# Returning the last expert pair's results inside the next norm's loop, with the branch for full experts ahead of that pair's down products

## The chip, the cores and the metric

The kernel runs on one core of a Trainium2 chip. The metric is the device time of one execution in microseconds (us). The core has five engines with queues of their own, each of which works strictly in the order of its program: PE (TensorE, matrix products; its weight loads are listed as PEld), DVE (VectorE), ACT (ScalarE), POOL (GpSimd) and SP (SyncE, which here only issues transfers). Engines wait for one another through semaphores.

## The reference

Two layers over x of 512 tokens by 1024 channels, float32. Layer 0 mixes the tokens with differential attention, layer 1 with stick-breaking attention, and a mixture of 32 experts follows each. Ahead of each of the four sub-layers x is normed by rows and modulated; behind it the result, times a gate, is added to x. At the end x is normed once more, with a gain:

```
def rms_norm(x, g, eps=RMS_EPS):
    xf = x.astype(jnp.float32)
    y = xf * lax.rsqrt(jnp.mean(xf * xf, axis=-1, keepdims=True) + eps)
    return (y * g.astype(jnp.float32)).astype(x.dtype)
```

Each token goes to the best two experts of the best of four groups, and each expert is `silu(x @ gate) * (x @ up) @ down`, weighted by its probability. No assignment is dropped, however many tokens choose one expert.

## The kernel before

**Tiles and pairs.** The 512 tokens are four tiles of 128 (`NT`), tile i of x being `xt(xs, i)`. `experts` (called once for each layer) works on the 32 experts in 16 pairs, 64 places for each expert. For a pair, `gate_up` makes gate and up products, `act_mul` the hidden values, `hid_transposed` turns them, `down` makes the down products (L1229, 16 products that the trace shows as 32, since each float32 product takes two passes), `slot_weights` and `slot_tokens` the matrix that maps places to tokens (its last operation is L1202 on DVE), and `scaled_parts` scales the result from PSUM (DVE, L1050) and splits it in two parts that the faster matrix format holds: `hi` on ACT (L1059) and `lo`, the remainder, on DVE (L1060).

**The return.** `combine` (L1069 and L1072) returns a group's results to the tokens: for one tile and one half of the channels, PE multiplies the place matrix by `hi` and by `lo` (L1069), and DVE adds the product to x (L1072). For the last pair that is 4 tiles x 2 halves, 16 products and 8 additions.

**The branch.** `overflow` (L1082) handles tokens beyond an expert's 64 places. It stands in a branch of the program that every engine takes together: each loads the count `nb` (L1088), and jumps over the body if it is zero (L1090), which it is in both layers of the profiled execution. No instruction is moved over the branch, and an engine leaves it only when the others' work before it that it depends on is done.

**The next norm.** After layer 0 the norm of layer 1 is done tile by tile in `norm_modulate_tile` (L451): the sum of squares on ACT (L400), the root on ACT (L404), a reciprocal and a Newton step of eight small operations for two tiles on DVE (L405 to L414), a diagonal matrix of the result (L456, DVE), 8 products that scale and transpose the tile at once (L460, PE, 16 passes in the trace), the modulation from PSUM (L469 on DVE, L467 on ACT), and again a split in `hi` (L472, ACT) and `lo` (L473, DVE). The first products of layer 1's attention (L556 to L558, its v projection, 24 for each tile) need these parts, and the split of their weights (L484 on ACT, L485 on DVE). x itself goes to the buffer `x2d` in memory (L1283). After layer 1 the final norm is done tile by tile (L1436 to L1445), and the last half tile's transfer to `out` ends the program.

**The order.** The order of each engine's program is made when the kernel is built: instructions are recorded, and a scheduler places each by what it depends on, within what `behind` and `chain` fix by hand. A branch closes such a stretch. The weights come over SP's queue in a fixed order (`fetch`, `release`, `reserve`); the last pair's down weights are 8 loads of 512 KB.

Of the kernel before, what the change touches and what calls it, by code (L numbers as in the profile page):

```python
# [9 lines left out]
F32 = mybir.dt.float32  # L10
# [27 lines left out]
def trunk_kernel(ctx: ExitStack, tc: tile.TileContext, io):  # L38
# [78 lines left out]
    def sl(s):  # L117
        return slots[:, s, :]
# [74 lines left out]
    def behind(inst, *others):  # L193
        for other in others:
            tc.add_manual_dep(inst.ins, other.ins.name, no_sync, reason="lesser work comes later")
# [203 lines left out]
    def row_sumsq(x_ap, junk, out):  # L399
        act.activation(junk, x_ap, AF.Square, accum_out=out)  # L400
# [50 lines left out]
    def norm_modulate_tile(i, xs, cols, ring4, ring2):  # L451
        ssq = small.tile([P, 1], F32, name="ssqt")
        row_sumsq(xt(xs, i), ring4(), ssq)
        r = rstd_of(ssq, 1, 1e-6, D)
        diag = ring2()[:, 0:P]
        diags.append(dve.tensor_scalar(diag, ident, r[:, 0:1], None, op0=ALU.mult))  # L456
        pt = sc_ps()
        full = ring4().rearrange("p (kb t) -> p kb t", kb=KB)
        for kb in range(KB):
            pe.matmul(pt[:, kb // 4, P * (kb % 4):P * (kb % 4) + P], lhsT=xt(xs, i)[:, P * kb:P * kb + P], rhs=diag,  # L460
                      start=(kb % 4 == 0), stop=(kb % 4 == 3))
        for kb in range(KB):
            c, j = kb % 4, kb // 4
            po = pt[:, j, P * c:P * c + P]
            a, b = cols[:, c, 2 + j:3 + j], cols[:, c, j:j + 1]
            if kb % 2:
                act.activation(full[:, kb, :], po, AF.Identity, scale=a, bias=b)  # L467
            else:
                dve.tensor_scalar(full[:, kb, :], po, a, b, op0=ALU.mult, op1=ALU.add)  # L469
        for j in range(2):  # L470
            hi, lo = (rs_(s[j]).rearrange("p (kb t) -> p kb t", kb=4)[:, :, P * i:P * i + P] for s in (R_HI, R_LO))
            last_a = act.activation(hi, full[:, 4 * j:4 * j + 4, :], AF.Copy)  # L472
            last_d = dve.tensor_tensor(lo, full[:, 4 * j:4 * j + 4, :], hi.bitcast(F32), op=ALU.subtract)  # L473
        return last_a, last_d


# [686 lines left out]
    def experts(l, st, xs, g2, hte_sl, w2, r2, ap, shp, rows, wrows):  # L1163
# [56 lines left out]
        def down(hidT):  # L1220
            pd = sc_ps()
            for hf in range(2):
                ws = [fetch(), fetch()]
                for f2 in range(2):
                    fb = 2 * hf + f2
                    for nn in range(2):
                        for e in range(2):
                            c0 = 1024 * f2 + 512 * nn
                            chain(pe.matmul(pd[64 * e:64 * e + 64, nn, :], lhsT=hidT[:, fb, 64 * e:64 * e + 64],  # L1229
                                            rhs=sl(ws[e])[:, c0:c0 + 512], start=(fb == 0), stop=(fb == 3)))  # L1230
                release(ws)
            return pd

        group = []
        for pr in range(np_):
            if pr == np_ - 1:
                reserve(5)
            pg = gate_up(pr)
            if pr == 0:
                wt = route_weights(st, w2, md)  # L1240
                token_rows(lambda c, i: st["sid"][:, c, i:i + 1], lambda: (r2(), ones_r), rows, (md,), True)
                token_rows(lambda c, i: wt[:, i, c:c + 1], lambda: (w2(), ones), wrows, (), True)
                sidq = small.tile([P, nq, 2, NT], F32, name="sidq", bufs=1)
                for qd in range(nq):
                    behind(dve.tensor_scalar(sidq[:, qd], st["sid"], float(-256 * qd), None, op0=ALU.add), md)
                ovf = route_overflow(st, w2)
            hid = act_mul(pg, slice(0, P), w2)
            units = []
            if pr % 2 and pr < np_ - 1:
                units = [lambda k2=k2: dispatch(k2) for k2 in range(KB // 2)]  # L1250
            elif pr:
                done, group = group, []
                units = [lambda i=i, nn=nn: combine(done, xs, i, nn) for i in range(NT) for nn in range(2)]
            if pr == np_ - 1:

                behind(act.activation(small.tile([P, 1], F32, name="table"), eps6, AF.Sqrt), *silu)
            half = len(units) // 2
            for u in units[:half]:
                u()
            hidT = hid_transposed(hid, P, w2, chain)  # L1260
            for u in units[half:]:
                u()
            pd = down(hidT)
            slotw = slot_weights(pr)
            group.append((slot_tokens(pr), scaled_parts(pd, slotw, g2, w2, r2)))
            if pr % 2 == 0 and pr < np_ - 2:
                for i in range(NT):
                    pick(sidq, i, pr // 2 + 1, sb, w2)
        overflow(l, st, ovf, wt, xs, g2, ap, shp, rows)
        for i in range(NT):  # L1270
            for nn in range(2):
                combine(group, xs, i, nn)


    sbs = [None]
    x2d = dram.tile([S, D], F32, name="x2d")
    for l in range(2):
        if l == 0:
            xsrc = x_v
        else:  # L1280
            xsrc = x2d.rearrange("(t p) d -> p t d", p=P)
            for s2 in range(2):
                nc.sync.dma_start(xsrc[:, 2 * s2:2 * s2 + 2, :], sl(x_sl[s2]).rearrange("p (t d) -> p t d", t=2))  # L1283
            xo_sl = alloc(2)
            work_sl = alloc(4)
        w4 = Ring(parts_of(slots, work_sl[0:3], 1024))
        w2 = Ring(parts_of(slots, work_sl[3:4], 512))
        if l == 0:
            ada_flush((0, 0), 2)
            neglam, sgc = late_loads()  # L1290
            norm_transposed(x_sl, xo_sl, w4)
        else:
            for i in range(NT):
                anchor[:] = norm_modulate_tile(i, x_sl, columns[1, 0], w4, w2)
        reserve(4)
        release(x_sl)
# [13 lines left out]
                order = ((0, 0), (1, 0), (0, 1), (1, 1), (2, 0), (2, 1))  # L1310
            units.append((g, order))
        linked.clear()
        holds = {(0, 2): (None, diags[1]), (0, 0): anchor} if l else {}
        line = Line([u for g, order in units for u in qkv_units(l, g, qkv_sl, order, chain)], holds)
        line.split(1)
        if l == 0:
# [106 lines left out]
        reserve(0)  # L1423
        w2 = Ring(parts_of(slots, work_sl[0:1], 512))
        rows, wrows = parts_of(rslots, (R_ROWS,), 512)[0:2], parts_of(slots, r_sl, 512)[0:2]
        experts(l, st, x_sl, g2, hte_sl, w2, r2, ap, shp, rows, wrows)
        reserve(8)
        release(hte_sl + r_sl + work_sl[0:1])

# [4 lines left out]
    ov = io["out"].rearrange("o (t p) d -> p (o t) d", p=P)  # L1434
    w4 = Ring(parts_of(slots, alloc(2), 1024))
    for i in range(NT):  # L1436
        ssq = small.tile([P, NT], F32, name="ssq")
        t = w4()
        row_sumsq(xt(x_sl, i), t, ssq[:, 0:1])
        r = rstd_of(ssq, 1, 1e-6, D)  # L1440
        n = 2 if i == NT - 1 else 1
        for c in range(n):
            cs_ = slice(D // n * c, D // n * c + D // n)
            dve.scalar_tensor_tensor(t[:, cs_], xt(x_sl, i)[:, cs_], r[:, 0:1], gf[:, cs_], op0=ALU.mult, op1=ALU.mult)  # L1444
            nc.sync.dma_start(ov[:, i, cs_], t[:, cs_])  # L1445


# [24 lines left out]
```

## Time and profile before

| | |
|---|---|
| median of 3 runs | 1587.94 us (1587.5 to 1588.52) |
| the profiled execution's own time | 1587.79 us |
| its span, first to last instruction | 1586.1 us |
| PE busy | 1510.2 us (95%) |
| DVE busy | 819.1 us (52%) |
| ACT busy | 456.2 us (29%) |
| POOL busy | 69.8 us (4%) |
| mean granted TensorE clock | 0.978 of full speed |

The span is 1.7 us shorter than the execution's own time; this lies around the span. Busy times overlap, so they don't add up to it. Layer 0 ends near 796 us, where the last L1229 of its experts is done, and layer 1's near 1564 us.

### The profile page before, as it was taken

The numbers are of one execution on the slowest core, as the hardware profiler recorded it, in microseconds if no ns is written. First come the engines' busy times: TensorE is split into PE (matmuls) and PEld (weight loads), VectorE is DVE, ScalarE is ACT, GpSimd is POOL, SyncE is SP. The second block draws the span as 40 slices with busy tenths as digits, with TensorE's granted clock in tenths as the row PEclk, the third lists the DMA queues.
The fourth block names the chain that finished last, engine by engine and source line by source line (L and its number), as shares of the span: only waits on it lengthen the run. The fifth ranks groups of instructions, "written<-read, shape, count | busy, mean of one in ns | idle before, by whom it ended". The sixth has DMA issues, their size and how long they took to land. (4 is left out here: it accounts for less than half of the span.)

```text
span 1586.1 us, 20509 instructions
## 1 busy us (share of the span) xinstructions
PE 1510.2 (95%) x8077; PEld 910.2 (57%) x8077; DVE 819.1 (52%) x1664; ACT 456.2 (29%) x830; POOL 69.8 (4%) x98
## 2 busy tenths in 40 slices
PE   4999989899999999999989999998999999999996
PEld 2887778754544545544467877885445545445542
DVE  5957845743443442442477787666342343343345
ACT  4564655521111101101164545453101111111112
POOL 0000000000000000000002223300000000000000
PEclk8999999989999999999989999998999999999997
DMA  9837734179999999999966455323999999999994
GB/s 379 314 130 273 257 132 156 40 262 418 421 421 421 422 420 422 421 421 421 399 211 239 147 186 187 133 88 122 415 421 421 420 422 421 421 421 421 421 414 169
DMA packets 111519, 501.63 MB, mean 316 GB/s; under 512 B 14832, under 2 KB 39440, under 8 KB 65336
## 3 DMA queue, kind: packets, MB, share of 16 engines
q1 hardware_dynamic: 109688, 498.01, 79.1%
q10 hardware_dynamic: 1728, 2.23, 0.4%
q8 instruction: 67, 1.10, 0.3%
q14 instruction: 36, 0.29, 0.1%
HBM read 495.97 MB, written 4.23 MB: 315 GB/s over the span
## 5 line engine op out<-in xcount | busy, mean ns | idle before, releaser
L1214 PE MATMUL banks<-slots 128*64 128x512 f32 x2048 | 453.1, 595 | 0.2 <-DMA slots<-in_expert_w_up_dram 0.2
L1214 PEld LDWEIGHTS banks<-slots 128*64 128x64 f32 x2048 | 156.3, 138 | 290.6 <-issue 276.4
L1229 PE MATMUL banks<-slots 128*64 128x512 f32 x1024 | 226.8, 595 | 1.4 <-ACT slots L1046 1.4
L1037 DVE TENSOR_TENSOR slots<-slots,banks 128x512 f32<-128x512 f32 x32 | 22.0, 687 | 272.3 <-PE banks L1214 272.3
L1069 PE MATMUL banks<-rslots 128*128 128x512 f32 x512 | 142.8, 424 | 10.6 <-DVEq L1090 5.3
L1229 PEld LDWEIGHTS banks<-slots 128*64 128x64 f32 x1024 | 70.7, 137 | 137.3 <-issue 130.6
L1050 DVE SCALAR_TENSOR_TENSOR slots<-banks,slotw,slots 128x512 f32<-128x512 f32 x64 | 45.1, 746 | 191.8 <-PE banks L1229 186.1
L1069 PEld LDWEIGHTS banks<-rslots 128*128 128x128 f32 x512 | 91.3, 194 | 62.6 <-DVE slots L1072 25.9
L1059 ACT ACTIVATE rslots<-slots 128x512 fp32r<-128x512 f32 x64 | 40.0, 631 | 301.3 <-DVE slots L1050 300.0
L1182 PEld LDWEIGHTS banks<-hot,rslots 128*128 128x128 f32 x896 | 109.1, 192 | 11.4 <-issue 11.4
L1182 PE MATMUL banks<-hot,rslots 128*128 128x256 f32 x896 | 114.5, 286 | 0.0
L1072 DVE TENSOR_TENSOR slots<-banks,slots 128x512 f32<-128x512 f32 x144 | 97.2, 688 | 25.6 <-PE banks L1069 25.6
L539 PE MATMUL banks<-rslots 128*128 128x512 f32 x256 | 104.0, 406 | 3.7 <-ACT rslots L447 3.7
L540 PE MATMUL banks<-rslots 128*128 128x512 f32 x256 | 100.9, 394 | 0.8 <-DVE rslots L448 0.8
L541 PE MATMUL banks<-rslots 128*128 128x512 f32 x256 | 100.9, 394 | 0.0
L485 DVE TENSOR_TENSOR rslots<-slots,rslots 128x1024 fp32r<-128x1024 f32 x64 | 78.2, 1234 | 27.5 <-ACT rslots L484 26.0
L934 ACT ACTIVATE slots<-banks,consts 128x256 f32<-128x256 f32 x64 | 35.6, 564 | 197.2 <-PE banks L1182 174.9
L331 DVE SCALAR_TENSOR_TENSOR slots<-slots,consts 128x1024 f32<-128x1024 f32 x70 | 87.4, 1281 | 7.0 <-DMA slots<-in_ada_w_dram 6.9
L484 ACT ACTIVATE rslots<-slots 128x1024 fp32r<-128x1024 f32 x64 | 66.9, 1056 | 58.6 <-PE banks L540 20.5
L556 PE MATMUL banks<-rslots 128*128 128x256 f32 x256 | 74.5, 291 | 0.7 <-ACT slots L545 0.6
L558 PE MATMUL banks<-rslots 128*128 128x256 f32 x256 | 73.2, 286 | 0.5 <-DVE rslots L473 0.5
L557 PE MATMUL banks<-rslots 128*128 128x256 f32 x256 | 73.1, 286 | 0.0
(240 smaller groups left out, 1920.1 us busy)
## 6 DMA issues: line engine op xcount, KB each, us to landing
slots<-in_expert_w_gate_dram SPq DMA_DIRECT2D x104, 1024.0 KB
slots<-in_expert_w_up_dram SPq DMA_DIRECT2D x104, 1024.0 KB
slots<-in_expert_w_down_dram SPq DMA_DIRECT2D x104, 1024.0 KB
slots<-in_ada_w_dram SPq DMA_DIRECT2D x48, 1024.0 KB
slots<-in_expert_w_gate_dram SPq DMA_DIRECT2D x48, 512.0 KB
slots<-in_expert_w_up_dram SPq DMA_DIRECT2D x48, 512.0 KB
slots<-in_expert_w_down_dram SPq DMA_DIRECT2D x48, 512.0 KB
slots<-in_diff_w_in_dram SPq DMA_DIRECT2D x12, 1024.0 KB
```

The costliest lines, as they stand in the source:

```text
L331: add = dve.scalar_tensor_tensor(acc[:, c_], sl(s)[:, c_], cs[:, kb:kb + 1], acc[:, c_], op0=ALU.mult, op1=ALU.add)
L485: j = dve.tensor_tensor(rs_(ls)[:, cs_], sl(s)[:, cs_], rs_(hs)[:, cs_].bitcast(F32), op=ALU.subtract)
L539: link(pe.matmul(pt, lhsT=wh[:, kb, :], rhs=rT(R_HI, kb), start=(kb == 0), stop=False))
L540: link(pe.matmul(pt, lhsT=wh[:, kb, :], rhs=rT(R_LO, kb), start=False, stop=False))
L541: link(pe.matmul(pt, lhsT=wl[:, kb, :], rhs=rT(R_HI, kb), start=False, stop=(kb == KB - 1)))
L556: link(pe.matmul(po, lhsT=rT(R_HI, kb, ts), rhs=wh[:, kb, :], start=(kb == 0), stop=False))
L558: link(pe.matmul(po, lhsT=rT(R_LO, kb, ts), rhs=wh[:, kb, :], start=False, stop=(kb == KB - 1)))
L1069: chain(pe.matmul(pt, lhsT=sT[:, P * i:P * i + P], rhs=parts[nn][part], start=(n + part == 0), stop=(n == len(group) - 1 and part == 1)))
L1072: dve.tensor_tensor(xn, pt, xn, op=ALU.add)
L1182: chain(pe.matmul(pt[:, 256 * kk:256 * kk + 256], lhsT=rT(r, kb, slice(P * i, P * i + P)), rhs=sb[:, i, :], start=(i == 0 and r == R_HI), ...
L1214: chain(pe.matmul(pg[64 * e:64 * e + 64, w, :], lhsT=hTe[:, kb, c0:c0 + 64], rhs=sl(ws[e])[:, 512 * kk:512 * kk + 512], start=(kb == 0), s ...
L1229: chain(pe.matmul(pd[64 * e:64 * e + 64, nn, :], lhsT=hidT[:, fb, 64 * e:64 * e + 64], rhs=sl(ws[e])[:, c0:c0 + 512], start=(fb == 0), sto ...
```

## The change

In each layer's last pair, the place matrix and the branch now come ahead of `down`, with the small operation that loads ACT's table for the square root behind the branch (it stood ahead of `hid_transposed`). `experts` no longer returns the last pair's results itself. It gives back a function `last(i)` that does so for tile i; the caller runs it at the start of each turn of the next norm's loop. In layer 1 the store of x to `x2d` follows tile by tile in that loop. In `norm_modulate_tile` the diagonal and `lo` go to GpSimd. In the final norm, tiles 0 and 1 are scaled on ACT and multiplied by the gain on GpSimd; tiles 2 and 3 stay on DVE, in halves.

```diff
@@ norm_modulate_tile
-        diags.append(dve.tensor_scalar(diag, ident, r[:, 0:1], None, op0=ALU.mult))
+        pool.tensor_scalar(diag, ident, r[:, 0:1], None, op0=ALU.mult)
...
-                dve.tensor_scalar(full[:, kb, :], po, a, b, op0=ALU.mult, op1=ALU.add)
+                last_d = dve.tensor_scalar(full[:, kb, :], po, a, b, op0=ALU.mult, op1=ALU.add)
...
-            last_d = dve.tensor_tensor(lo, full[:, 4 * j:4 * j + 4, :], hi.bitcast(F32), op=ALU.subtract)
+            pool.tensor_tensor(lo, full[:, 4 * j:4 * j + 4, :], hi.bitcast(F32), op=ALU.subtract)
+        diags.append(last_d)
         return last_a, last_d
@@ experts
-            if pr == np_ - 1:
-
-                behind(act.activation(small.tile([P, 1], F32, name="table"), eps6, AF.Sqrt), *silu)
...
-            pd = down(hidT)
-            slotw = slot_weights(pr)
-            group.append((slot_tokens(pr), scaled_parts(pd, slotw, g2, w2, r2)))
+            if pr == np_ - 1:
+
+                slotw, sT = slot_weights(pr), slot_tokens(pr)
+                overflow(l, st, ovf, wt, xs, g2, ap, shp, rows)
+
+                behind(act.activation(small.tile([P, 1], F32, name="table"), eps6, AF.Sqrt), *silu)
+                pd = down(hidT)
+            else:
+                pd = down(hidT)
+                slotw, sT = slot_weights(pr), slot_tokens(pr)
+            group.append((sT, scaled_parts(pd, slotw, g2, w2, r2)))
...
-        overflow(l, st, ovf, wt, xs, g2, ap, shp, rows)
-        for i in range(NT):
+        def last(i):
             for nn in range(2):
                 combine(group, xs, i, nn)
+        return last
@@ layer 1, norm ahead of attention
-            for s2 in range(2):
-                nc.sync.dma_start(xsrc[:, 2 * s2:2 * s2 + 2, :], sl(x_sl[s2]).rearrange("p (t d) -> p t d", t=2))
...
             for i in range(NT):
+                last(i)
+                nc.sync.dma_start(xsrc[:, i, :], xt(x_sl, i))
                 anchor[:] = norm_modulate_tile(i, x_sl, columns[1, 0], w4, w2)
...
-        holds = {(0, 2): (None, diags[1]), (0, 0): anchor} if l else {}
+        holds = {(0, 2): (None, diags[0]), (0, 0): anchor} if l else {}
@@ final norm
     for i in range(NT):
-        ssq = small.tile([P, NT], F32, name="ssq")
+        last(i)
+        ssq = small.tile([P, 1], F32, name="ssqt")
         t = w4()
-        row_sumsq(xt(x_sl, i), t, ssq[:, 0:1])
+        row_sumsq(xt(x_sl, i), t, ssq)
         r = rstd_of(ssq, 1, 1e-6, D)
-        n = 2 if i == NT - 1 else 1
-        for c in range(n):
-            cs_ = slice(D // n * c, D // n * c + D // n)
+        if i < 2:
+            act.activation(t, xt(x_sl, i), AF.Copy, scale=r[:, 0:1])
+            pool.tensor_tensor(t, t, gf, op=ALU.mult)
+            nc.sync.dma_start(ov[:, i, :], t)
+            continue
+        for c in range(2):
+            cs_ = slice(512 * c, 512 * c + 512)
             dve.scalar_tensor_tensor(t[:, cs_], xt(x_sl, i)[:, cs_], r[:, 0:1], gf[:, cs_], op0=ALU.mult, op1=ALU.mult)
-            nc.sync.dma_start(ov[:, i, cs_], t[:, cs_])
+            if i == NT - 1 or c:
+                at = cs_ if i == NT - 1 else slice(0, D)
+                nc.sync.dma_start(ov[:, i, at], t[:, at])
```

In the changed kernel the lines from L457 to about L1250 have numbers one higher, so that L1069, L1072, L1229 and L485 of before are L1070, L1073, L1230 and L486; the orders below keep each kernel's own numbers. The rows between the jump and the end of the branch's body, which is not run, are left out.

First, PE at the end of layer 0, before:

```order
L1069 MATMUL banks<-rslots 128x512 x8
L1044 MATMUL banks<-consts,slots 128x128 x4
L1069 MATMUL banks<-rslots 128x512 x8
L1229 MATMUL banks<-slots 64x512 x16
L1088 TENSOR_LOAD nb
L1090 COMPARE_AND_BRANCH
...
L1090 UNCONDITIONAL_BRANCH
L1069 MATMUL banks<-rslots 128x512 x16
L460 MATMUL banks<-slots 128x128 x16
L556 MATMUL banks<-rslots 128x256
```

and in the change:

```order
L1070 MATMUL banks<-rslots 128x512 x8
L1045 MATMUL banks<-consts,slots 128x128 x4
L1070 MATMUL banks<-rslots 128x512 x8
L1089 TENSOR_LOAD nb
L1091 COMPARE_AND_BRANCH
...
L1091 UNCONDITIONAL_BRANCH
L1230 MATMUL banks<-slots 64x512 x16
L1070 MATMUL banks<-rslots 128x512 x16
L460 MATMUL banks<-slots 128x128 x24
L557 MATMUL banks<-rslots 128x256
```

The last pair's down products have moved behind the branch, and three tiles of the norm's products, where there were two, stand ahead of the first 22 v products; the fourth tile's follow these.

Second, ACT at the same place, before:

```order
L1256 ACT_TABLE_LOAD
L1256 ACTIVATE table<-consts 128x1
L1046 ACTIVATE slots<-banks 128x512
L1059 ACTIVATE rslots<-slots 128x512
L1088 TENSOR_LOAD nb
L1090 COMPARE_AND_BRANCH
...
L1059 ACT_TABLE_LOAD
L1059 ACTIVATE rslots<-slots 128x512
L484 ACTIVATE rslots<-slots 128x1024 x2
L400 ACTIVATE slots,ssqt<-slots 128x1024
L404 ACT_TABLE_LOAD
L404 ACTIVATE rstd<-ssqt,consts 128x1
```

and in the change:

```order
L1047 ACTIVATE slots<-banks 128x512
L485 ACTIVATE rslots<-slots 128x1024
L1089 TENSOR_LOAD nb
L1091 COMPARE_AND_BRANCH
...
L1266 ACT_TABLE_LOAD
L1266 ACTIVATE table<-consts 128x1
L485 ACTIVATE rslots<-slots 128x1024
L1060 ACTIVATE rslots<-slots 128x512 x2
L400 ACTIVATE slots,ssqt<-slots 128x1024
L404 ACTIVATE rstd<-ssqt,consts 128x1
```

Both halves of `hi` now stand behind the branch, no table load stands among them or ahead of the first root, and one split of v weights (L485, L484 of before) stands ahead of the branch. At the end of layer 1 ACT's order is the same without the two splits.

Third, GpSimd in layer 1's norm, in the change (before, only the fills L696 stood there):

```order
L456 TENSOR_SCALAR slots<-consts,rstd 128x128 x3
L473 TENSOR_TENSOR rslots<-slots,rslots 128x4x128 x2
L696 MEMSET slots 128x2
L473 TENSOR_TENSOR rslots<-slots,rslots 128x4x128
L696 MEMSET slots 128x2
L473 TENSOR_TENSOR rslots<-slots,rslots 128x4x128
L696 MEMSET slots 128x2
L456 TENSOR_SCALAR slots<-consts,rstd 128x128
L473 TENSOR_TENSOR rslots<-slots,rslots 128x4x128 x2
```

The fourth tile's diagonal (L456) stands behind the first two tiles' four subtractions (L473).

## Rows read from the trace of the kernel before

**Rows 1.** Windows: each engine's busy time, granted clock and DMA share, layer 1.
```profile
core 0: us, PE busy (x) PEld busy (x) DVE busy (x) ACT busy (x) POOL busy (x), PEclk, DMA share, GB/s
830.00:900.00 70.00, 69.31 (x394) 54.97 (x393) 57.03 (x60) 35.91 (x52) 20.55 (x23) 1.00 0.60 211
1200.00:1550.00 350.00, 348.53 (x1744) 168.14 (x1744) 131.60 (x254) 43.29 (x73) 0.00 (x0) 1.00 1.01 420
```

**Rows 2.** Timeline of PE, end of layer 0 and start of layer 1.
```profile
start us, us, engine line op out<-in xcount [idle before <-releaser]
788.52 7.09 PE L1229 MATMUL banks<-slots 128*64 128x512 f32 x32
798.22 1.01 PE L1069 MATMUL banks<-rslots 128*128 128x512 f32 x2 [2.62 <-DVEq L1090]
808.45 5.46 PE L460 MATMUL banks<-slots 128*128 128x128 f32 x32 [1.80 <-DVE slots L456]
817.69 3.74 PE L460 MATMUL banks<-slots 128*128 128x128 f32 x32
821.18 0.36 PE L558 MATMUL banks<-rslots 128*128 128x256 f32 x1
829.89 0.28 PE L558 MATMUL banks<-rslots 128*128 128x256 f32 x1
```

**Rows 3.** Timeline of DVE, the same stretch.
```profile
789.23 0.74 DVE L1202 SCALAR_TENSOR_TENSOR rslots<-rslots,consts,slots 128x512 fp32r<-128x512 f32 x1
795.72 1.41 DVE L1050 SCALAR_TENSOR_TENSOR slots<-banks,slotw,slots 128x512 f32<-128x512 f32 x2 [5.75 <-PE banks L1229]
797.17 0.69 DVE L1060 TENSOR_TENSOR rslots<-slots,rslots 128x512 fp32r<-128x512 f32 x1
800.19 0.68 DVE L1072 TENSOR_TENSOR slots<-banks,slots 128x512 f32<-128x512 f32 x1
806.68 0.69 DVE L1072 TENSOR_TENSOR slots<-banks,slots 128x512 f32<-128x512 f32 x1 [0.15 <-PE banks L1069]
808.12 0.48 DVE L456 TENSOR_SCALAR slots<-consts,rstd 128x128 f32<-128x128 f32 x2
808.51 1.22 DVE L485 TENSOR_TENSOR rslots<-slots,rslots 128x1024 fp32r<-128x1024 f32 x1
```

**Rows 4.** Timeline of ACT, the same stretch.
```profile
785.99 0.60 ACT L1046 ACTIVATE slots<-banks 128x512 f32<-128x512 f32 x1 [8.17 <-PE banks L1044]
799.46 1.99 ACT L484 ACTIVATE rslots<-slots 128x1024 fp32r<-128x1024 f32 x2
803.10 1.28 ACT L404 ACT_TABLE_LOAD   x1
804.60 1.04 ACT L400 ACTIVATE slots<-slots 128x1024 f32<-128x1024 f32 x1
805.97 1.04 ACT L400 ACTIVATE slots<-slots 128x1024 f32<-128x1024 f32 x1
```

**Rows 5.** Windows, the last pair's return at the end of layer 0.
```profile
799.20:807.50 8.30, 6.97 (x15) 3.31 (x14) 6.24 (x13) 7.44 (x13) 0.00 (x0) 0.64 0.32 126
```

**Rows 6.** Line L670 on GpSimd and on DVE: durations in ns, minimum/median/maximum.
```profile
L670 POOL TENSOR_TENSOR slots<-slots,rs x6: 1040/1040/1042, 112.2 to 217.1; 128x512 f32<-128x512 f32 x6
L670 DVE TENSOR_TENSOR slots<-slots,rs x2: 691/691/691, 248.4 to 267.3; 128x512 f32<-128x512 f32 x2
```

**Rows 7.** Timeline of DVE, end of the program: after the last down products.
```profile
1564.10 1.41 DVE L1050 SCALAR_TENSOR_TENSOR slots<-banks,slotw,slots 128x512 f32<-128x512 f32 x2 [5.75 <-PEq L1090]
1580.90 1.41 DVE L1444 SCALAR_TENSOR_TENSOR slots<-slots,rstd 128x512 f32<-128x512 f32 x2
```

**Rows 8.** Timeline of SP, transfers issued at both ends.
```profile
770.79 10.31 SPq L133 DMA_DIRECT2D slots<-in_expert_w_down_dram  x8
791.49 0.35 SPq L136 DMA_DIRECT2D slots<-in_ada_w_dram  x1
1577.60 5.07 SPq L1445 DMA_DIRECT2D out_dram<-slots  x5
```

More of the change, by code (lines that the diff above doesn't have):

```diff
@@ L1425, in trunk_kernel @@
         rows, wrows = parts_of(rslots, (R_ROWS,), 512)[0:2], parts_of(slots, r_sl, 512)[0:2]
-        experts(l, st, x_sl, g2, hte_sl, w2, r2, ap, shp, rows, wrows)
+        last = experts(l, st, x_sl, g2, hte_sl, w2, r2, ap, shp, rows, wrows)
         reserve(8)
```

## The prediction

> **What bounds the kernel now.** I read the windows first. In layer 1's attention and over its experts PE is busy 99% of the time at a granted clock of 1.00 [rows 1]; the transfers are full beside it in the experts, but the list of waits has none of PE on them there. So a microsecond that PE gains before 830 us should still be there at the end, and one that it loses too. Next come the two ends, in the timelines. In this text T is the start of the first scaling L1050, right behind the last L1229: 795.72 in layer 0 [rows 3], 1564.10 in layer 1 [rows 7].
>
> Behind T, PE waits 2.62 us at the branch [rows 2]. The first addition to x starts at 800.19, T + 4.47, the last ends at 807.37, T + 11.65 [rows 3]; ACT loads a table for 1.28 us between the first sum of squares and its root [rows 4], and the clock averages 0.64 in the stretch [rows 5]. L460 starts at 808.45, T + 12.7, and the 96 v products, with the norm's last two tiles between them, end at 829.89 + 0.12, T + 34.3 [rows 2]. At the end of the program the last scaling by DVE ends at 1582.31, T + 18.2 [rows 7], and the span 3.8 us later, for the last half tile's store and the end of the program. These two lengths, 34.3 and 18.2 us, are what the change can shorten.
>
> **The cost: the branch before the down products.** It now stands where PE would go straight on. DVE comes to it only behind L1202, which ends at 789.97 [rows 3]. From the end of DVE's last operation before the branch (797.17 + 0.69) to PE's first product behind it (798.22) took 0.36 us [rows 2, 3], so the down products go on at 790.33. All but the first two now stand behind DVE's branch; the third started at 788.52 + 2 x 0.22 = 788.96. That is 1.4 us later. The same operations stand at the end of layer 1, so I count it twice: **+2.8 us**. Nothing hides it, since PE stands on the path there. Bounds: 0.9 (the products that run early cover part) and 3.6 us (0.4 more at each branch, as long again as the 0.36).
>
> ACT must be at the branch too: L1046 ends at 786.59 [rows 4], and in layer 0 one split of v weights now stands behind it (two took 1.99 us, so 1.0 each [rows 4]), which gives 787.6 and is hidden behind DVE's 789.97, if its weights are in by 788.9. SP also takes the branch earlier, with four (layer 0) or two (layer 1) of the down loads behind it. Before, the eighth load was issued near 780.8 and must be in by 791.49, where SP passes its branch: at most 10.7 us in a full queue [rows 8]. Now SP passes once the first of them are in: the second piece, third in line behind a load of double size, is issued near 770.8 + 2 x 1.4 = 773.6 and lands near 786. The fifth piece, issued next, is wanted at 790.3 + 4 x 0.89 = 793.9, so over 7 us remain for a queue that is by then nearly empty. I take nothing.
>
> **The return.** Behind T nothing but data is waited for. From T: the two scalings take 1.41; `hi` of the first half is done at 797.17 - 795.72 = 1.45 as now; the second follows on ACT without table load; DVE's two `lo` at 0.69 run from 1.45 to 2.83. The first addition, behind them on DVE, starts at T + 2.85 instead of 4.47. The eight then need between 8 x 0.69 = 5.5 us (DVE without a gap) and the 7.2 us of before (807.37 - 800.19, at the low clock): the last ends between 8.4 and 10.0, I take 9.4.
>
> **The norm of layer 1.** The first tile's Newton step is placed behind the seventh addition, 8.6. A 128x128 operation on GpSimd isn't in the trace: between a quarter of L670's 1.04 us (it has a quarter of the elements) and all of it [rows 6], I take 0.5. So L460 starts near 9.3 instead of 12.7. Three tiles at 3.74 / 2 (full clock) to 5.46 / 2 us (as the first two ran) [rows 2] are 5.6 to 8.2 us; I take 6.5: 15.8. Then 22 v products at (829.89 - 821.18) / 73 = 0.12 us: 18.4. The fourth tile's diagonal waits on GpSimd behind four subtractions. These have L670's form and size: 1.04 us, against 0.69 on DVE [rows 6]. The first `hi` is there at about 12.7 (half a tile of L460, four modulations, a split), so the four, their fills and the diagonal end at 12.7 + 4 x 1.1 + 0.8 = 17.9, just before PE wants it. With L460's fourth tile (1.9) and 74 products (8.9) the v products end at **T + 29.2**; as 9.3 can be up to 0.6 later and the diagonal may wait too, I take 29.6, with bounds of 28.8 and 30.6. Gain: 34.3 - 29.6 = **4.7 us** (3.7 to 5.5).
>
> The Trainium skill (GPSIMD Engine Reference, section 4.1, Engine selection) speaks against this part: element by element work with two inputs belongs on VectorE, GpSimd being about twice slower. The ratio in [rows 6] is 1.5. By the page a subtraction would take about 1.4 us (an estimate, twice 0.69), the fourth diagonal would come 1.3 us later, and the gain would be 3.4.
>
> **The final norm.** The sums of squares follow each tile's second addition, 1.4 us apart with their root (804.60 to 805.97 [rows 4]). The third ends at 8.9 to 9.5; two scalings on ACT at 1.04 (as L400) end at 11.0 to 11.6; root 0.3 and Newton step 0.75 (807.37 to 808.12 [rows 3]) give 12.1 to 12.7; DVE's two halves take 1.41 [rows 7], the fourth tile's Newton step behind them 0.5, its halves 1.41: T + 15.4 to 16.0 instead of 18.2. Gain 2.2 to 2.8, I take **2.5 us**. GpSimd's products of 128x1024 (2 x 1.04 = 2.1 us; at least 1.04, at most 4.2, twice as much again) end at 10 + 4.2 = 14.2, ahead of that. Stores in four pieces instead of two, and the moved place matrix, cost nothing: SP had waited for additions there anyway, and L1202's place on DVE doesn't move.
>
> **Sum.** 2.8 - 4.7 - 2.5 = -4.4 us. On the profiled execution's own 1587.79 us (span 1586.1 and 1.7 around it) that is 1583.4; it lies 0.15 below the median of the three runs, so **1583.5 us**, with its own range of 1581.5 to 1585.5.
>
> **The rivals.** (1) *GpSimd is too slow, which ends on the other side: slower.* If a subtraction takes s us, the v products end 4 us later for each us of s over 1.04, and above s = 1.4 the two final products, 2s each, hold back the stores: 10 + 4s for the 15.7. With s = 2.08, the v products end at 29.2 + 4.2 = 33.4, a gain of 0.9, and the last product at 18.3, a gain of none: 2.8 - 0.9 = +1.9, 1589.8 us. It turns slower above s = 1.8. [Rows 6] speak against it, six times within 2 ns, but say nothing of what DVE did beside them. The Trainium skill (SBUF — State Buffer, section SBUF: two separate sides) has a rule for it: an operation of VectorE with two SBUF inputs and one of GpSimd that reads SBUF shut each other out for their whole length. A lock of this kind would add part of DVE's L485, 1.22 us each [rows 3], of which two stand between tile 0 and the fourth diagonal: 2.4 us at most, so 1585.9, not slower. Chance of slower by this way 0.08, of the milder form with 1585 to 1587 0.14.
>
> (2) *A load holds the branch of layer 0.* ACT's split ahead of it waits for v weights, which are now issued second among the down loads, near 772.2. With 10.7 us in the queue and a piece of double size they land near 784. Each us after 788.9 delays the down products by one; if they came at 793.7, about 5 us late, 1588.3: no change. The queue's row speaks against it. Chance 0.06.
>
> (3) *The gain of layer 1's norm is taken back.* What follows the v products would have to wait for weights or for DVE instead: 1583.5 + 3.3 = 1586.8, no change. For it: the transfers' share of 0.60 to 1.01; against it: PE's 99% [rows 1]. Chance 0.17.
>
> **How the numbers follow.** My forecast has 0.45, and 0.10 is left for more than it, below 1581.5 (the clock at 1.00 throughout, additions without gaps). 0.2%, 3.2 us, is about what a measurement of this kernel can tell from no change. Faster by more than that: 0.10, 0.42 of the forecast, 0.05 of the milder form of (1) and 0.02 of the others: 0.59. Slower by more: half of (1)'s slower form, 0.04, where the branch also takes its upper bound, 0.02 for a load in (2) that comes over 8 us late, 0.01 for (3): 0.07. The rest, 0.34, is within. For 8 in 10 the range runs from 1580.8 (both gains at their upper bound, 5.5 + 2.8, and the branch at 1.3) to 1588.0, which takes in (2), (3) and the milder (1).
>
> **What would show it.** Right: a gap of some 1.4 us ahead of L1230's third product at both ends, and none at a branch behind it; first addition at T + 2.9; no table load behind T; L473 on GpSimd near 1.04; v products ending near T + 29.6; DVE's last scaling near T + 15.7; the windows of layer 1 as before. Wrong: a longer gap at the branch, with ACT or SP last; L473 over 1.3 us; PE waiting for the fourth diagonal; waits of PE on weights after 830.

## The result

| | before | changed |
|---|---|---|
| median | 1587.72 us (4 runs, 1585.05 to 1588.52) | 1601.85 us (4 runs, 1600.33 to 1602.6) |
| ratio | | 1.0093, 95% interval 1.0079 to 1.0107 |
| span of the profiled execution | 1586.1 us | 1600.4 us |

The change is slower by 14 us, where 4.4 us less was forecast. PE in the changed kernel's timeline (columns as in [rows 2]):

```profile
797.31 9.81 PE L1230 MATMUL banks<-slots 128*64 128x512 f32 x32 [6.74 <-PEq L1091]
808.70 0.50 PE L1070 MATMUL banks<-rslots 128*128 128x512 f32 x1 [1.57 <-ACT rslots L1060]
...
816.92 5.62 PE L460 MATMUL banks<-slots 128*128 128x128 f32 x48 [0.99 <-POOL slots L456]
825.43 0.39 PE L558 MATMUL banks<-rslots 128*128 128x256 f32 x1 [0.83 <-DVE rslots L486]
828.73 2.52 PE L460 MATMUL banks<-slots 128*128 128x128 f32 x16 [1.97 <-POOL slots L456]
...
840.90 0.28 PE L559 MATMUL banks<-rslots 128*128 128x256 f32 x1
...
1568.93 3.01 PE L1230 MATMUL banks<-slots 128*64 128x512 f32 x10 [0.42 <-PEq L1091]
1573.60 5.36 PE L1230 MATMUL banks<-slots 128*64 128x512 f32 x22 [1.67 <-issue]
```

VectorE at the same places:

```profile
791.22 0.74 DVE L1203 SCALAR_TENSOR_TENSOR rslots<-rslots,consts,slots 128x512 fp32r<-128x512 f32 x1
807.23 1.41 DVE L1051 SCALAR_TENSOR_TENSOR slots<-banks,slotw,slots 128x512 f32<-128x512 f32 x2 [15.27 <-PE banks L1230]
810.08 0.69 DVE L1073 TENSOR_TENSOR slots<-banks,slots 128x512 f32<-128x512 f32 x1
816.06 0.68 DVE L1073 TENSOR_TENSOR slots<-banks,slots 128x512 f32<-128x512 f32 x1
823.36 0.87 DVE L413 TENSOR_TENSOR nwt<-nwt,rstd 128x1 f32<-128x1 f32 x1
...
1590.99 2.26 DVE L413 TENSOR_TENSOR nwt<-nwt,rstd 128x1 f32<-128x1 f32 x1
1595.66 1.41 DVE L1455 SCALAR_TENSOR_TENSOR slots<-slots,rstd 128x512 f32<-128x512 f32 x2
```

From before to after, by these rows against [rows 2, 3, 7]: 2.0 us are lost before the change's first place (L1202 starts at 789.23 before, L1203 at 791.22 after, behind the same work); another 6.8 until the down products start (788.52, now 797.31); 2.7 in them, as they take 9.81 us instead of 7.09. From T to the last v product 33.8 us instead of 34.3: a gain of 0.5. The attention and the experts of layer 1 add 0.5, and the branch ahead of layer 1's down products another 0.5. These products take 10.0 us with a hole of 1.67 in them, 2.9 more. Behind them 0.7 us are gained. That makes 14.2 of the span's 14.3 us. The first 2.0 lie within what single executions differ by: the kernel with only a new final norm (below), whose program is the same as before up to there, has its first down product at 791.69 in its profiled execution, 3.2 us later than before.

The two windows on either side of the late start show the clock (columns as in [rows 1]):

```profile
790.50:797.30 6.80, 0.08 (x1) 0.02 (x1) 1.46 (x3) 1.67 (x3) 0.00 (x0) 0.65 0.57 226
797.30:807.20 9.90, 9.81 (x32) 3.17 (x32) 0.00 (x0) 0.00 (x0) 0.00 (x0) 0.72 0.93 317
```

PE does nothing for 6.7 us, the granted clock falls on the way, and the down products then run at 0.72 on average: that is the 2.7 us.

What does PE wait for? It is its own queue, at the branch. The changed kernel's lines of the branch for PE and, to compare, for DVE (durations in ns, minimum/median/maximum, then the first and last start):

```profile
L1091 DVEq COMPARE_BRANCH  x2: 56/64/72, 791.2 to 1568.9; - x2
L1091 PEldq COMPARE_BRANCH  x2: 426/3492/6557, 790.4 to 1568.2; - x2
L1091 PEldq EVENT_SEMAPHORE  x2: 51/51/51, 797.1 to 1568.7; - x2
```

and before, a row that I had not weighed:

```profile
L1090 PEldq COMPARE_BRANCH  x2: 3825/4985/6145, 791.8 to 1560.0; - x2
```

At layer 0 PE's jump over the branch's body takes 6.6 us now and took 6.1 us before. Then it began while the queue still held down products until 795.6, so only 2.3 us of it were seen. DVE takes 0.06 us for the same jump. The transfers of the changed kernel in two stretches within PE's jump, 790.5 to 794.4 us first, then 794.4 to 797.3 us (packets, MB, share of 16 engines), point to what it waits for:

```profile
q1 hardware_dynamic: 409, 1.49, 96.3%
q14 instruction: 1, 0.01, 0.5%
...
q1 hardware_dynamic: 13, 0.02, 2.2%
q8 instruction: 1, 0.02, 2.1%
```

A block of code (queue 8, 16 KB) comes only in the second stretch, from 794.7 to 795.7 us by the trace's packets, and 1.3 us later the jump is over. In the kernel before, at both layers, the jump ends 1.4 to 1.5 us behind such a block. That this block is PE's is read off these times; the rows don't name its engine. The Trainium skill (Runtime: NRT & Kernel Launch, section Instruction fetch mechanics) says that code is fetched ahead in blocks in sequence only, and that a taken branch to code outside the current two blocks must first load the target's. The rows agree; how long it takes the page doesn't say.

### The profile page after: what moved, and what is told of

Same layout as the page of the kernel before. It is cut to its first block, busy times and chain, and to the rows that moved or that the text cites. A ratio compares the mean times of both kernels' runs of the same rounds, so it can differ in the third digit from the quotient of the medians.

```text
span 1600.4 us, 20500 instructions
## 1 busy us (share of the span) xinstructions
PE 1514.0 (95%) x8077; PEld 909.2 (57%) x8077; DVE 817.5 (51%) x1651; ACT 453.7 (28%) x828; POOL 89.3 (6%) x112
## 5 line engine op out<-in xcount | busy, mean ns | idle before, releaser
L1230 PE MATMUL banks<-slots 128*64 128x512 f32 x1024 | 230.8, 601 | 10.2 <-PEq L1091 7.2
L1230 PEld LDWEIGHTS banks<-slots 128*64 128x64 f32 x1024 | 71.8, 138 | 149.2 <-issue 141.3
L1070 PE MATMUL banks<-rslots 128*128 128x512 f32 x512 | 139.5, 414 | 8.8 <-DVE slots L1073 4.7
L1070 PEld LDWEIGHTS banks<-rslots 128*128 128x128 f32 x512 | 89.4, 190 | 59.5 <-DVE slots L1073 25.0
L1073 DVE TENSOR_TENSOR slots<-banks,slots 128x512 f32<-128x512 f32 x144 | 97.2, 689 | 23.3 <-PE banks L1070 23.1
L486 DVE TENSOR_TENSOR rslots<-slots,rslots 128x1024 fp32r<-128x1024 f32 x64 | 78.7, 1243 | 27.2 <-ACT rslots L485 25.9
L485 ACT ACTIVATE rslots<-slots 128x1024 fp32r<-128x1024 f32 x64 | 67.0, 1056 | 62.6 <-PE banks L541 21.5
```

The source lines that it names most:

```text
L486: j = dve.tensor_tensor(rs_(ls)[:, cs_], sl(s)[:, cs_], rs_(hs)[:, cs_].bitcast(F32), op=ALU.subtract)
L1070: chain(pe.matmul(pt, lhsT=sT[:, P * i:P * i + P], rhs=parts[nn][part], start=(n + part == 0), stop=(n == len(group) - 1 and part == 1)))
L1073: dve.tensor_tensor(xn, pt, xn, op=ALU.add)
```

## The experiments

Each kernel is compared with the kernel before on the same chip, whose median was 1587.3 to 1588.7 us. Single executions of one kernel spread by up to 11.5 us, so the medians of 6 to 12 runs and their intervals carry the verdicts. The profiles, one execution each, show the places.

**The change with the branch back behind the scaling**

```diff
-                slotw, sT = slot_weights(pr), slot_tokens(pr)
-                overflow(l, st, ovf, wt, xs, g2, ap, shp, rows)
...
+        overflow(l, st, ovf, wt, xs, g2, ap, shp, rows)
+
         def last(i):
```

> The changed kernel with one part undone: the branch stands behind the last pair's down products and scaling again, and the table operation where it was before. Theory of the jump (PE needs 4 to 7 us to get its code behind the branch's body, hidden before by 7 us of down products in its queue): the 6.6 us pause and the 2.7 us of half clock at layer 0 and 2.9 us at layer 1 go, about 1.5 us of waiting at each branch behind the down products come back: 1588 to 1593 us. Theory that the loss lies in the norm on GpSimd: still above 1597 us.

Measured: 1592.26 us, 1.0029 (1.0017 to 1.004). The 9.6 us that come back are the branch's; 4 us of loss remain that are not its.

**The branch alone, in the kernel before**

```diff
+            if pr == np_ - 1:
+                slotw, sT = slot_weights(pr), slot_tokens(pr)
+                overflow(l, st, ovf, wt, xs, g2, ap, shp, rows)
...
+                pd = down(hidT)
```

> The kernel before with one part of the change: place matrix, branch and table operation ahead of the last pair's down products; return, norm and final norm as before. Theory of the jump: 9.3 us lost at layer 0 and 2.9 us at layer 1, about 1.5 us less behind the products at each: 1595 to 1599 us. Theory that the branch costs what I forecast (1.4 us each) and the rest is lost elsewhere: 1586 to 1589 us.

Measured: 1595.18 us, 1.0047 (1.0028 to 1.0067): 7.1 us slower, as the theory of the jump has it. VectorE and PE in it:

```profile
807.02 1.41 DVE L1050 SCALAR_TENSOR_TENSOR slots<-banks,slotw,slots 128x512 f32<-128x512 f32 x2 [15.10 <-PE banks L1229]
809.76 1.35 DVE L1072 TENSOR_TENSOR slots<-banks,slots 128x512 f32<-128x512 f32 x2
816.74 3.84 PE L460 MATMUL banks<-slots 128*128 128x128 f32 x32 [1.81 <-DVE slots L456]
836.62 0.28 PE L558 MATMUL banks<-rslots 128*128 128x256 f32 x1
```

With return and norm as before, the first addition starts at T + 2.7, L460 at T + 9.7, and the v products end at T + 29.7. So moving the branch away from behind T gives by itself the T + 29.6 that I had put down to the return tile by tile and to GpSimd in layer 1's norm; the jump costs more than that. How much of the gain from T + 34.3 is the branch's is not sharp: the kernel with only a new final norm, with the same program there as before, has T + 32.3 in its profiled execution.

**A short body**

```diff
-            with tc.For_i(0, nbv, 1) as bi:
...
+            t = wo()
+            dve.tensor_copy(t[0:n, :], rows[0].bitcast(F32)[0:n, :])
+            for k in range(2):
+                pg = sc_ps()
+                pe.matmul(pg[0:n, 0, :], lhsT=t[0:n, 0:n], rhs=t[0:n, :], start=True, stop=True)
+                dve.tensor_copy(t[0:n, :], pg[0:n, 0, :])
```

> The changed kernel with the body of the branch cut to a few instructions (the work for full experts, which is not run with these inputs, is left out); branch and all else stay where the change puts them. Theory of the jump: the code behind a short body is already at hand, so PE's pause ahead of the down products shrinks from 6.7 us to about 1.5 us at layer 0, and the 2 us hole among them at layer 1 may go: 1588 to 1593 us. Rival, PE waits for the other engines or for the loads behind SP's branch: pause and time as in the changed kernel, 1600 to 1602 us.

Measured: 1590.7 us, 1.0017 (1.0007 to 1.0028): 11 us below the changed kernel, with the branch, the loads behind it and the other engines' work at the same places. Its branch line and its down products:

```profile
L1091 PEldq COMPARE_BRANCH  x2: 207/215/223, 788.1 to 1556.5; - x2
```

```profile
789.84 7.09 PE L1173 MATMUL banks<-slots 128*64 128x512 f32 x32 [1.55 <-DVEq L1091]
```

The jump takes 0.2 us, PE waits 1.55 us, now for VectorE, as I had forecast (1.4), and the down products run in 7.09 us. So the pause comes with the length of the body that is jumped, not from the other engines or SP's loads. (In the kernel with the branch alone moved, the profile names a load of down weights as what released these products at 797.44. But the jump's row ends at 797.1 there, and with the short body the loads stand behind the same branch and hold nothing up.)

**The return tile by tile without GpSimd**

```diff
-        pool.tensor_scalar(diag, ident, r[:, 0:1], None, op0=ALU.mult)
+        dve.tensor_scalar(diag, ident, r[:, 0:1], None, op0=ALU.mult)
...
-            pool.tensor_tensor(lo, full[:, 4 * j:4 * j + 4, :], hi.bitcast(F32), op=ALU.subtract)
+            last_d = dve.tensor_tensor(lo, full[:, 4 * j:4 * j + 4, :], hi.bitcast(F32), op=ALU.subtract)
```

with the branch back as in the first, and the final norm's four tiles on VectorE.

> The changed kernel with the branch back behind the down products and all of GpSimd's new work on VectorE again (final norm: all four tiles in halves on VectorE); what remains is the return tile by tile. Theory that GpSimd and VectorE shut each other out: faster than the same kernel with GpSimd's work by 2 to 6 us, and 1 to 4 us below the kernel before: 1583.5 to 1587 us. Rival, VectorE gets too much: no faster than with GpSimd.

Measured: 1593.03 us, 1.0031 (1.002 to 1.0042): no faster than with GpSimd, so the theory of GpSimd seemed to fall. PE in its timeline:

```profile
821.38 0.58 PE L558 MATMUL banks<-rslots 128*128 128x256 f32 x1 [4.03 <-DVE rslots L486]
```

PE waits 4 us for the second split of v weights on VectorE. The change holds this split behind `diags[0]`, the first tile's last operation on VectorE; here that is a subtraction, later still. What this row shows is a loss by order, not by the return itself. **With the branch between products and scaling** it was the same:

> The changed kernel without GpSimd's new work, and with the branch (and the table operation behind it) between the last pair's down products and their scaling, so that PE's jump has 7 us of products ahead of it. Theory that the return tile by tile itself loses (three tiles of L460 ahead of the first v products, and the split of v weights late on VectorE): the kernel with the tiles only, less 4 to 6 us of table loads and waiting at the branch: 1587 to 1590 us. Rival, that kernel lost at its branch: 1582 to 1585 us.

Measured: 1593.15 us, 1.0038 (1.0026 to 1.0051), with the same wait of 4.0 us.

**The branch between the down products and their scaling, nothing else**

```diff
-            if pr == np_ - 1:
-
-                behind(act.activation(small.tile([P, 1], F32, name="table"), eps6, AF.Sqrt), *silu)
...
             pd = down(hidT)
-            slotw = slot_weights(pr)
-            group.append((slot_tokens(pr), scaled_parts(pd, slotw, g2, w2, r2)))
+            slotw, sT = slot_weights(pr), slot_tokens(pr)
+            if pr == np_ - 1:
+                overflow(l, st, ovf, wt, xs, g2, ap, shp, rows)
+
+                behind(act.activation(small.tile([P, 1], F32, name="table"), eps6, AF.Sqrt), *silu)
+            group.append((sT, scaled_parts(pd, slotw, g2, w2, r2)))
...
-        overflow(l, st, ovf, wt, xs, g2, ap, shp, rows)
```

> The kernel before with only the branch, and the table operation behind it, put between the last pair's down products and their scaling; return, norm and final norm as before. Theory of the jump: its 4 to 7 us lie behind the down products in PE's queue, and without table loads and without scaling ahead of the branch the 4.6 and 1.8 us that the branch-only kernel gained behind its products at layers 0 and 1 are kept for the most part: 1581 to 1585 us. Rival, PE still comes out of the jump too late, since its sequencer runs only 4 us ahead of the queue: 1586 to 1588 us.

Measured: 1586.12 us, 0.9992 (0.9982 to 1.0001): no difference, as the rival had it. ACT, the branch line and PE in it:

```profile
791.70 1.06 ACT L484 ACTIVATE rslots<-slots 128x1024 fp32r<-128x1024 f32 x1 [4.77 <-SPq L1090]
```

```profile
L1090 PEldq COMPARE_BRANCH  x2: 3345/4656/5968, 794.8 to 1561.8; - x2
```

```profile
800.98 7.57 PE L1069 MATMUL banks<-rslots 128*128 128x512 f32 x16 [4.81 <-PEq L1090]
```

ScalarE waits 4.8 us ahead of its branch. The row names SP's branch, which SP had passed at 786.7; what the split needs are v weights, issued at 779.8, so I read it as a wait for them. PE's jump starts 5.9 us behind the first down product (788.86) instead of 3.3 us (788.52 and 791.8 before). So this split goes behind the branch:

```diff
-                behind(act.activation(small.tile([P, 1], F32, name="table"), eps6, AF.Sqrt), *silu)
+                tabs.append(act.activation(small.tile([P, 1], F32, name="table"), eps6, AF.Sqrt))
+                behind(tabs[-1], *silu)
...
-        holds = {(0, 2): (None, diags[1]), (0, 0): anchor} if l else {}
+        holds = {(0, 2): (tabs[0], diags[1]), (0, 0): anchor} if l else {}
```

> The kernel with the branch between the last pair's down products and their scaling, and in addition the first split of v weights on ScalarE held behind the table operation, so that no load is waited for ahead of the branch. Theory: PE came out of the jump at 800.98 there because ScalarE, waiting for the v weights, came to the branch 2.6 us late; now PE is out near T + 2.5 at layer 0, the table loads stay off the path, and 3 to 6 us are gained on the kernel before: 1582 to 1585 us. Rival, the jump alone is too long at layer 0: no better than with the split ahead, 1586 to 1587 us.

Measured: 1585.06 us, 0.9982 (0.9973 to 0.9991), 3.6 us below the kernel before. The intervals of this kernel and the one ahead of it overlap, so the step between the two is read from the traces. PE in this one:

```profile
L1091 PEldq COMPARE_BRANCH  x2: 3505/5005/6505, 792.9 to 1557.8; - x2
```

```profile
789.61 7.09 PE L1230 MATMUL banks<-slots 128*64 128x512 f32 x32
799.52 1.16 PE L1069 MATMUL banks<-rslots 128*128 128x512 f32 x4 [2.82 <-PEq L1091]
```

PE's jump starts 3.3 us behind the first down product again, and PE's wait there falls from 4.8 to 2.8 us.

**GpSimd alone, in the kernel before**, first in layer 1's norm, then in the final norm, with the diffs of the change. The first of them moves the hold of the split of v weights to `diags[0]` too, as the change does.

> The kernel before with only the diagonals and subtractions of layer 1's norm on GpSimd. Theory that GpSimd and VectorE hold each other up: 1 to 4 us slower than before, 1589 to 1592 us, with subtractions of over 1.5 us where VectorE works beside them. Rival, the relief of VectorE is worth as much: 1587 to 1588.5 us.

Measured: 1591.41 us, 1.0028 (1.0018 to 1.0038). PE waits 3.9 us in three places for GpSimd's diagonals in its trace, and 1.5 us for the split that is held.

> The kernel before with only the new final norm (two tiles scaled on ScalarE and multiplied on GpSimd, two in halves on VectorE), all results returned ahead of it as before. Theory that they hold each other up: GpSimd's products at 2.3 us keep VectorE's Newton step waiting as in the changed kernel, 0 to 2 us slower: 1588 to 1590 us. Rival, two engines share the work: 1 to 2 us faster, 1586 to 1587 us.

Measured: 1591.02 us, 1.0018 (1.0006 to 1.003). Both lose. VectorE and GpSimd in the second:

```profile
1577.62 0.28 DVE L413 TENSOR_TENSOR nwt<-nwt,rstd 128x1 f32<-128x1 f32 x2
1581.64 2.26 DVE L413 TENSOR_TENSOR nwt<-nwt,rstd 128x1 f32<-128x1 f32 x1
```

```profile
1579.24 4.64 POOL L1443 TENSOR_TENSOR slots<-slots 128x1024 f32<-128x1024 f32 x2 [550.38 <-ACT slots L1442]
```

The same operation on one number a row takes 0.14 us alone (two in 0.28) and 2.26 us beside GpSimd's second product (2.3 us, until 1583.88).

**Tiles with the old hold, then GpSimd on top**

```diff
-        for i in range(NT):
+        def last(i):
             for nn in range(2):
                 combine(group, xs, i, nn)
+        return last
```

on the kernel with the split behind the branch, which is "the kernel before it" in the first of the two expectations here; `diags[1]`, the second tile's diagonal, stays the hold.

> The kernel before it in this list, and in addition the return tile by tile in both norms, with all of the norm's work on VectorE and the split of v weights held behind the second tile's diagonal as before, not behind the first tile's modulation. Theory that the tile kernels lost by their order (the late split, three tiles of L460 ahead of the first v products): with the old hold it is as fast as without tiles or up to 2 us faster: 1581 to 1585 us. Rival, the return tile by tile itself loses: 2 to 5 us slower than without.

Measured: 1581.95 us, 0.9962 (0.9951 to 0.9973): the fastest of all, 6.8 us below the kernel before. PE in it:

```profile
798.24 7.58 PE L1069 MATMUL banks<-rslots 128*128 128x512 f32 x16 [3.02 <-PEq L1091]
806.87 3.84 PE L460 MATMUL banks<-slots 128*128 128x128 f32 x32 [1.06 <-DVE slots L456]
```

Two tiles of L460 (32 passes) stand ahead of the v products again, not three (48), and the wait of 4 us is gone. No run shows what the hold alone is worth: the kernel with the 4 us wait at 1593.15 us differs from this one also in the place of the first split and in the final norm's halves. Of the 10.9 us between their traces from the first down product on, 6.6 lie between the down products and the last v product. Nor do the traces show where the 3.1 us come from by which the return tile by tile betters the kernel without it: from the first down product on the two profiled executions take 791.3 and 791.6 us.

> The kernel before it in this list with the diagonals and subtractions of layer 1's norm on GpSimd, and the hold as in the change. Theory that GpSimd and VectorE hold each other up: 2 to 5 us slower than with VectorE alone, 1585 to 1589 us. Rival, they work side by side: within 1 us of it.

Measured: 1586.2 us, 0.9989 (0.9977 to 1.0). GpSimd's part, with the hold that the change ties to it, costs 4.2 us there. PE's rows tell the two apart, 0.84 us for the split that is held and 2.29 for GpSimd ahead of the fourth tile (the row names a fill, L697, that runs beside the fourth diagonal):

```profile
814.41 0.39 PE L558 MATMUL banks<-rslots 128*128 128x256 f32 x1 [0.84 <-DVE rslots L486]
817.55 2.82 PE L460 MATMUL banks<-slots 128*128 128x128 f32 x16 [2.29 <-POOL slots L697]
```

**The change with only the branch and the first split placed so**, all of its other parts kept:

> The changed kernel with one edit: the branch (and the table operation) between the last pair's down products and their scaling, and the first split of v weights behind it; return tile by tile, GpSimd's work in both norms as in the change. Theory that the branch's place makes most of the loss: 12 to 15 us faster than the changed kernel, 1587 to 1590 us, that is the kernel with the tiles and GpSimd in layer 1's norm (1586.2 us) and 1 to 3 us for GpSimd in the final norm. Rival, the tiles and GpSimd lose more together than in the runs so far: above 1592 us.

Measured: 1588.49 us, 1.0001 (0.9989 to 1.0013). One edit takes 13.4 of the 14.1 us back; what remains of the change is worth nothing on the whole. From the kernel at 1586.2 us this one differs by GpSimd's part in the final norm alone, and is 2.3 us slower.

## Why the prediction was wrong

**The branch: the step that failed.** I wrote that from the end of DVE's last operation before the branch to PE's first product behind it took 0.36 us, and that the down products would go on 1.4 us later. I also let the first two of them run ahead of the branch, though the order of the change has all 16 behind it; this would have made it 1.8 us. The 0.36 us hold only where PE has already made its jump. Before, the jump of 6.1 and 3.8 us ran below the down products in the queue, work that the change puts behind it: the cover itself was moved. Measured are 6.8 us of delay and 2.7 us of low clock at layer 0, and at layer 1 0.5 us of delay and 2.9 in products with a hole: 13 for the forecast 2.8. The body's length decides (short body: 0.2 us), and the transfers show the code coming. Why the jump is longer at layer 0 is argued, not shown: its transfers are at 0.96, and a block of code may queue behind the weights. There the block's transfer starts 4.3 us behind the jump's start; in the kernel before, at layer 1, where the transfers are at 0.015, it starts 1.4 us behind it and the jump takes 3.8. In the change, at layer 1, a block had come by 1568, the jump took 0.43 us, and the hole (1571.9 to 1573.6) falls where the next block comes (1571.3 to 1572.3).

**The sum.** Forecast were -4.4 us, the rows give +14.2. Of the 18.6 between them the branch has 10.1, the norm of layer 1 4.2, the final norm 1.8, the late start of the profiled execution 2.0, and layer 1's attention and experts 0.5.

**The return: right, but not by the return tile by tile.** First addition forecast at T + 2.85, measured 810.08 - 807.23 = 2.85; last one at T + 9.4, measured 9.5. The kernel with the branch alone moved has its first addition at T + 2.7: what it takes is that no branch and no table load stand behind T.

**The norm of layer 1: the milder form of rival (1) came, and cost more.** L460 began at T + 9.7 (9.3), and its three tiles took 5.62 us (6.5). But the v products ended at T + 33.8, not 29.6; the kernel with the branch alone moved has them at T + 29.7, so the other parts of the change took 4 us of that gain back here. GpSimd in the changed kernel:

```profile
816.26 0.60 POOL L456 TENSOR_SCALAR slots<-consts,rstd 128x128 f32<-128x128 f32 x1 [34.82 <-DVE nwt L412]
821.01 3.21 POOL L473 TENSOR_TENSOR rslots<-slots,rslots 128x512 fp32r<-128x512 f32 x2 [1.64 <-ACT rslots L472]
824.21 2.30 POOL L473 TENSOR_TENSOR rslots<-slots,rslots 128x512 fp32r<-128x512 f32 x1
826.67 1.26 POOL L473 TENSOR_TENSOR rslots<-slots,rslots 128x512 fp32r<-128x512 f32 x1
828.07 0.61 POOL L456 TENSOR_SCALAR slots<-consts,rstd 128x128 f32<-128x128 f32 x1
...
1588.59 4.64 POOL L1450 TENSOR_TENSOR slots<-slots 128x1024 f32<-128x1024 f32 x2 [549.89 <-ACT slots L1449]
```

The diagonal's 0.5 us was near (0.60). A subtraction takes 1.26 us, not 1.04 (its result is fp32r, that of L670 f32; whether this makes the difference no run shows), and up to 2.3 us with VectorE at work beside it. The fourth diagonal ended at T + 21.4 instead of 17.9: the first subtraction started 1.1 us later than I had it, and the four took 6.9 us with their fills, not 4.4. PE waited 1.97 us, and its clock fell again behind the wait (L460's 16 passes took 2.52 us there, not 1.9, and the first v products 0.21 us each, not 0.12). Rival (1) in its milder form had this mechanism, at 2.4 us at most; I gave it 0.14 and took the undisturbed 1.04 us for the sum. The late start and the fall of the clock stood in no term. The Trainium skill (SBUF — State Buffer, section SBUF: two separate sides) has the lock as a rule, and the traces agree in both directions. In the kernel with the branch back, VectorE's and GpSimd's rows say it most plainly:

```profile
827.91 4.56 DVE L331 SCALAR_TENSOR_TENSOR slots<-slots,consts 128x1024 f32<-128x1024 f32 x2
834.66 2.47 DVE L331 SCALAR_TENSOR_TENSOR slots<-slots,consts 128x1024 f32<-128x1024 f32 x2
```

```profile
822.50 2.50 POOL L473 TENSOR_TENSOR rslots<-slots,rslots 128x512 fp32r<-128x512 f32 x2
827.32 4.07 POOL L473 TENSOR_TENSOR rslots<-slots,rslots 128x512 fp32r<-128x512 f32 x2 [2.26 <-ACT rslots L472]
```

Side by side (from 827.3) each pair takes about as long as both together, 4.6 and 4.1 us; apart, 2.5 and 2.5.

**The final norm: the same.** DVE ended at 1597.07, T + 18.0, not 15.7. GpSimd's products took 2.3 us (2.1), and that alone would have been hidden; but VectorE's Newton step stood still beside them, 2.26 us in one operation. I had looked for what GpSimd's result delays, not for what it blocks.

**What PE gains or loses stays: right.** The 11.0 us that were lost at the end of the v products were 12.0 at the last down products, of which 0.5 are the branch's.

**The other rivals.** The load that holds ScalarE's branch (2) did not come in the change, where L485 had run by 789.5; it did come in the kernel with the branch between, whose loads stand in the old order: there PE's jump starts 2.6 us later than without it, and PE waits 2.0 us longer behind its products. The gain taken back (3) had nothing to act on in the change. In the kernel with the tiles and the branch between, one of the two with the 4 us wait, it shows in layer 1's attention, and the other has it too (1.95 us):

```profile
870.83 2.38 PE L771 MATMUL banks<-slots 128*64 128x256 f32 x24 [1.78 <-DVE slots L746]
```

## What to carry to other kernels

A wait of 0.4 us behind a branch says what the branch costs only while its jump is covered: before moving one, look at the branch instruction's own row on the engine that is moved, and ask what lies in that engine's queue. Put a branch where the longest engine has work queued and the others are idle, here between products and their scaling, and keep loads from being waited for ahead of it. Work that goes to a second engine is free only if it doesn't hold the first one up; price it by a row in which both work.

## What the runs showed that I had not expected

PE's jump over this body takes 3.3 to 7.1 us in most of its places in these kernels. It takes 0.4 us at layer 1 of the two kernels with the branch ahead of the down products, where a block of code had come before it, and 0.2 us over a short body. An operation of VectorE on 128x1 took 2.26 us, fifteen times its own length, beside GpSimd. With the norm on VectorE, a hold moved from the second tile's diagonal to the first tile's last operation goes with a wait of 4 us on PE for a split of weights. And the branch's move, which I had counted as a cost only, brought by itself the gain that I had forecast for the rest.
